# Norm multiplication and low parts of the activations on GpSimd, and another place for ScalarE's first moves, in a one-core decoder layer

## Chip, cores and metric

One core of one Trainium2 chip runs the whole layer as one program. The metric is the device time of one execution in microseconds (us); lower is better. The engines are called by the profile's names: PE (TensorE), DVE (VectorE), ACT (ScalarE), POOL (GpSimd) and SP (SyncE, whose queue issues nearly all DMAs). PEld is the weight load of PE.

## The reference, cut to what matters

The program is one conditioned decoder layer for 256 tokens of width 2048. What bears on the change is its opening: the modulation from the conditioning vector, the first norm, and the big projection `w_in` of 12288 columns.

```python
def modulate(h, shift, scale):
    return h * (1.0 + scale[:, None, :]) + shift[:, None, :]

mod = jax.nn.silu(c) @ w_ada[l] + b_ada[l]
shift1, scale1, gate1, shift2, scale2, gate2 = jnp.split(mod, 6, axis=-1)
h = modulate(rms_norm(x, g_norm1[l]), shift1, scale1)
p = h @ w_in[l]
```

All of it is float32. Behind it stand retention, HGRN2, an output projection, and a feed-forward part with a causal convolution, which the change leaves alone.

## The kernel before, in words

Activations lie transposed: 16 k tiles, each of 128 channels on the partitions and 256 tokens along the row. Four tiles `xT` hold x, four k tiles in each.

**A product in three parts.** Each float32 operand is split in two for PE. A weight block arrives by DMA in a `raw` buffer (11 of them). ACT copies it, rounded, into the upper part `wh` (L176); DVE subtracts, `wl = raw - wh` (L181, in `rest`). There are four buffers each for `wh` and `wl`. An activation tile `hT` has an upper part in its first 256 columns and a low part in the next 256. PE adds upper times `wh`, low times `wh` and upper times `wl`: L205, L206 and L210 where the tokens are on the output's rows, L221, L222 and L225 where they are on its columns. In L205 and L206 the two alternate: the low part of a k tile is read right behind its upper part.

**Where an activation tile comes from.** For each k tile, the columns of `w_ada` for scale and shift arrive in four pieces. DVE multiplies each with silu(c) and adds up (L507, "dot"): two dots give the scale, two the shift. ACT makes of them the scale `s1` (L518, L519) and the shift `t1` (L524). In `modulated`, ACT writes the upper part of `hT` (L434), then the same value unrounded into `h` (L435), and DVE writes the low part, h minus upper (L436). Before that, x is multiplied by the norm factor of its token, `rx_sb` (L497, in `times`): k tiles 0 and 1 one at a time in the opening, the later ones in seven pairs by DVE, from inside the generator `ada1`, which makes one k tile.

**The order of the work.** The first 12 column groups of `w_in` (`ATT`, of 512 columns each) are visited in turns, while the activation tiles are still being made. `visits` lays out the turns: one visit takes a group as many k tiles further as are ready by the plan (about one new tile in 11 units of work). Groups 0 to 3 are opened by hand in `run` with k tiles 0 and 1. The visits begin with group 4, at first with two k tiles, then three, then four. `self.finish(*ada[:have])` at the head of a visit traces whatever is missing of the k tiles that it needs. In this phase `self.ordered` is False: a scheduler orders the instructions by their place in the trace and by their dependencies, and a few manual ones hold it. At the end of a group's first visit ACT moves the sums from PSUM to SBUF (`take`, L880: the first moves, "p<-pg"). A first move is held behind `self.upped`, the last part that ACT made and that was traced ahead of it; both `upper` and `modulated` set `self.upped`. When the visit was a group's first, a second `finish` (L1016 and L1017) traces the k tiles of the next visit before this move. The multiplication of a pair and the dots are held behind `self.last`, the last `wl`.

POOL does almost nothing: four constants at the start and four MEMSETs of tiles that the HGRN2 part uses.

Of the kernel before, what the change touches and what calls it, by code (L numbers as in the profile page):

```python
# [12 lines left out]
F32 = mybir.dt.float32  # L13
# [3 lines left out]
AF = mybir.ActivationFunctionType  # L17
ALU = mybir.AluOpType

P = 128  # L20
D = 2048
T = 256
NT = T // P
KT = D // P
# [12 lines left out]
NOSYNC = mybir.DependencyInfo(mybir.DependencyClass.NoSync, mybir.DependencyReason.DATA)  # L37
# [23 lines left out]
class Kernel:  # L61
# [368 lines left out]
    def modulated(self, dst, x, k, sc, sh):  # L430

        act = self.nc.scalar.activation
        h = self.s1([P, T], name="h")
        self.pin(act(dst[:, :T], x, AF.Identity, bias=sh[:, k : k + 1], scale=sc[:, k : k + 1]))  # L434
        self.upped = self.pin(act(h, x, AF.Identity, bias=sh[:, k : k + 1], scale=sc[:, k : k + 1]))  # L435
        self.pin(self.nc.vector.tensor_tensor(dst[:, T:], h, dst[:, :T].bitcast(F32), ALU.subtract))  # L436

    def turn_rows(self, ps, x, k, diag, t):

# [406 lines left out]
    def run(self):  # L846
        nc, a = self.nc, self.a
        c = self.consts
# [10 lines left out]
        def act(k):  # L859
            return hT[k // 2][:, k % 2, :]  # L860

        def ada1(k):
            if k > 0 and k % 2 == 0:
                ins = self.times(k, 2, rx_sb)
                self.tc.add_manual_dep(ins.ins, self.last.ins.name, NOSYNC, reason="behind the weights traced ahead of it")
            yield from self.scale_shift("ada1", k, s1, t1, self.gn1)
            if k % 2 == 0:
                hT[k // 2] = self.blk([P, 2, 2 * T], F32R, name="hT")
            self.modulated(act(k), self.xT[k // 4][:, k % 4, :], k, s1, t1)
            yield 0.7  # L870

        accs = [self.blk([P, NT, G] if c0 in ROWS else [P, 4, T], name="p") for c0 in ATT]
        done = [0] * len(ATT)
        mms = [self.mm_rows if c0 in ROWS else self.mm_cols for c0 in ATT]

        def take(g, ps, fresh):
            for at, z in self.parts(ps, ATT[g] in ROWS):
                dst = accs[g][:, at, :]
                if fresh:
                    ins = nc.scalar.activation(dst, z, AF.Copy)  # L880
                    self.tc.add_manual_dep(ins.ins, self.upped.ins.name, NOSYNC, reason="behind the parts traced ahead of it")
                else:
                    nc.vector.tensor_tensor(dst, dst, z, ALU.add)
# [10 lines left out]
        def opening(k):  # L894
# [3 lines left out]
            return z  # L898

        ada = [None, None, *(ada1(k) for k in range(2, KT))]  # L900
        gen = first(0)
        for _ in range(2):
            next(gen)
        rx = self.token_rstd(parts)
        rx_sb = c.tile([P, T], F32, name="rx_sb")
# [6 lines left out]
        h = self.s1([P, T], name="h")  # L912
# [25 lines left out]
        h = self.s1([P, T], name="h")  # L938
# [6 lines left out]
        for g in range(RESIDENT, FIRST):  # L945
            wh, wl = self.rest(self.upper(a["wa"][g][:, 1:2, :], 1, G, shift=COLS))
            mms[g](ps[g], [(act(1), wh[:, 0, :], wl[:, 0, :])], False, True)
        begun = list(self.pieces(a["wa"][FIRST][:, 0:2, :], 2))
        stock = {g: self.load(a["wa"][g][:, 0:2, :], 2, G) for g in range(FIRST + 1, FIRST + 4)}
        for _ in range(2):  # L950
# [11 lines left out]
        def visit(g):  # L962
            return COLS if g in cols else (0, 0)
# [3 lines left out]
        def begin(kind, hb, *ins):  # L967
            att.append(self.start(kind(hb, *ins, gates)))

        def visits():  # L970
            work, g = sum(done), FIRST
            seen = list(done)
            while min(seen) < KT:
                have = min(KT, 2 + int((work - LAG) / ADA_EVERY))
                m = have - seen[g]
                if m > 0:
                    yield g, m, work
                    seen[g] = have
                    work += m
                else:  # L980
                    work += 0.5
                g = (g + 1) % len(ATT)
                if have == KT and seen[0] < KT:
                    g = min(i for i in range(len(ATT)) if seen[i] < KT)

        def early(g, m):
            k = done[g]
            pieces = self.pieces(a["wa"][g][:, k : k + m, :], m, shift=visit(g), raw=stock.pop(g, None))
            return chain([next(pieces)], pieces)

        small = False
        plan = list(visits())
# [3 lines left out]
        for n, (g, m, work) in enumerate(plan):  # L996
            if work > SMALL and not small:
                small = True
                self.small_loads(nc.sync, ("freq", "lbT", "lmask"))
                self.start(self.trig())  # L1000
                self.start(self.lower_bound())
            fresh = done[g] == 0
            have = done[g] + m
            self.finish(*ada[:have])
            bank = ps[g] if g < RESIDENT else self.pg()
            whole = g >= RESIDENT
            ahead = early(*plan[n + 1][:2]) if m <= 2 and n + 1 < len(plan) else None
            if n == 0:
                for i in range(RESIDENT, FIRST):
                    take(i, ps[i], True)  # L1010
            if g == FIRST + 2 and fresh:
                self.pace(1, 4, ADA_EVERY / 2)
            self.products(mms[g], bank, a["wa"][g], act, done[g], m, first=whole, last=whole or have == KT, shift=visit(g), begun=begun)
            done[g] = have
            begun = ahead or (early(*plan[n + 1][:2]) if n + 1 < len(plan) else None)
            if fresh and n + 1 < len(plan):  # L1016
                self.finish(*ada[: done[plan[n + 1][0]] + plan[n + 1][1]])  # L1017
            if whole or have == KT:
                take(g, bank, fresh or not whole)
            if have == KT and ATT[g] in GATES:  # L1020
                nc.scalar.activation(accs[g], accs[g], AF.Silu)
                gates[GATES.index(ATT[g])] = accs[g]
            for hb in range(2):
                gs = [hb, 2 + hb, 4 + hb]
                if g in gs and min(done[i] for i in gs) == KT:
                    self.pace(0, 14.0, 24)
                    begin(self.hgrn, hb, *(accs[i] for i in gs))
                    for i in gs:
                        accs[i] = None
# [92 lines left out]
        def half(j, t):  # L1122

            return self.modulated_half(turned[j], 2 * j, self.sc2, self.sh2, t)
# [6 lines left out]
        for t in range(NT):  # L1131
            self.residual(x1[3], ps, g, None, 3, t)
            if t == 1:
                h = half(0, 0)
# [272 lines left out]
```

## Time and profile before

| what | value |
|---|---|
| time, median of 3 runs (lowest, highest) | 1504.11 us (1503.45, 1504.54) |
| the profiled execution: its own time | 1503.49 us |
| its span, from first to last instruction | 1501.7 us |
| granted TensorE clock, mean | 0.997 |
| PE busy | 1486.4 us, 99% of the span |
| DVE busy | 1206.5 us, 80% |
| ACT busy | 835.3 us, 56% |
| POOL busy | 4.0 us, 8 instructions |

In each row of a time line stand the start of the instruction in us from the span's start, its duration (or that of a run of like instructions, with their count behind the x), the engine, the line of the kernel, the operation and its tiles as out<-in, and in square brackets how long the engine had been idle before it and who ended this. Engines overlap their instructions somewhat: a row of 1.22 us on DVE is followed by the next after 1.14 us. The end of a matmul is modelled.

### The profile page before, as it was taken

What the parts mean: (1) busy time and instruction counts of PE and PEld (TensorE: products, weight loads), DVE (VectorE), ACT (ScalarE), POOL (GpSimd) and SP (SyncE); (2) the same over time, 40 slices, a digit from 0 to 9 for tenths busy, and PEclk for the clock granted to TensorE, in tenths of its full rate; (3) what the DMA queues carried; (4) which work ended last, traced back from release to release, by engine and by line L of the source; (5) the groups of instructions that cost most, each with busy time, mean ns of one, the idle gap of its engine ahead of it and who ended that gap; (6) DMA issues with size and microseconds to landing.
All of it is one profiled execution on the core that took longest, in us unless ns stands there. A gap on an engine that the chain in (4) does not pass through costs nothing.

```text
span 1501.7 us, 22778 instructions
## 1 busy us (share of the span) xinstructions
PE 1486.4 (99%) x8529; PEld 1275.6 (85%) x8529; DVE 1206.5 (80%) x1647; ACT 835.3 (56%) x1204; POOL 4.0 (0%) x8
## 2 busy tenths in 40 slices
PE   9999999999999999999999999999999999999997
PEld 8788898888888888888888888888888888888886
DVE  7799996999999877898978778778777769455694
ACT  5646446767775644445466555555555558344342
POOL 0000000000000000000000000000000000000000
PEclk9999999999999999999999999999999999999999
DMA  9999997778887889989847777777777666666551
GB/s 364 374 336 340 317 325 261 259 259 277 277 284 265 280 299 328 314 289 363 306 131 241 249 232 233 234 234 238 232 247 233 222 188 207 196 210 209 180 186 56
DMA packets 111167, 385.73 MB, mean 257 GB/s; under 512 B 12832, under 2 KB 13392, under 8 KB 111056
## 3 DMA queue, kind: packets, MB, share of 16 engines
q1 hardware_dynamic: 110160, 383.14, 76.1%
q8 instruction: 67, 1.10, 0.3%
q10 hardware_dynamic: 896, 1.13, 0.2%
q14 instruction: 44, 0.36, 0.1%
HBM read 382.11 MB, written 2.11 MB: 256 GB/s over the span
## 4 chain that ended last, share of the span: by engine, by line
PE 91%; DVE 4%; ACT 2%; issue 1%; DMA 1%; DVEq 0%; ACTq 0%
PE pg L205 12%; PE pg L206 12%; PE pg L210 12%; PE po L1240 11%; PE pg L1240 11%; PE po L1242 5%; PE pg L1242 5%; PE pg L255 4%; PE po L205 3%; PE po L210 3%; PE po L206 3%; PE pg L258 2%; DVE wl L181 2%; DVE raw L507 2%; ACT wh L176 1%
## 5 line engine op out<-in xcount | busy, mean ns | idle before, releaser
L181 DVE TENSOR_TENSOR wl<-raw,wh 128x1024 fp32r<-128x1024 f32 (+1 forms) x531 | 630.0, 1196 | 224.3 <-ACT wh L176 215.4
L176 ACT ACTIVATE wh<-raw 128x1024 fp32r<-128x1024 f32 (+1 forms) x531 | 544.3, 1037 | 465.0 <-PE pg L206 188.0
L507 DVE SCALAR_TENSOR_TENSOR raw<-raw,sc 128x1024 f32<-128x1024 f32 (+2 forms) x194 | 233.5, 1209 | 1.7 <-DMA raw<-in_ada 1.7
L205 PE MATMUL pg<-wh,hT 128*128 128x512 f32 x512 | 202.4, 395 | 3.2 <-ACT wh L176 2.5
L206 PE MATMUL pg<-wh,hT 128*128 128x512 f32 x512 | 199.6, 390 | 0.0
L1240 PE MATMUL po<-h2T,wh 128*128 128x512 f32 x704 | 175.8, 392 | 0.0
L1240 PE MATMUL pg<-h2T,wh 128*128 128x512 f32 x688 | 172.1, 392 | 0.0
L1240 PEld LDWEIGHTS po<-h2T,wh 128*128 128x128 f32 x704 | 125.7, 188 | 21.7
L1240 PEld LDWEIGHTS pg<-h2T,wh 128*128 128x128 f32 x688 | 122.8, 188 | 21.2
L210 PE MATMUL pg<-wl,hT 128*128 128x512 f32 x512 | 138.2, 389 | 0.0
L205 PEld LDWEIGHTS pg<-wh,hT 128*128 128x128 f32 x512 | 96.1, 188 | 24.4 <-ACT wh L176 3.3
L210 PEld LDWEIGHTS pg<-wl,hT 128*128 128x128 f32 x512 | 96.1, 188 | 20.3
L206 PEld LDWEIGHTS pg<-wh,hT 128*128 128x128 f32 x512 | 96.2, 188 | 19.2
L1242 PEld LDWEIGHTS po<-h2T,wl 128*128 128x128 f32 x704 | 93.4, 188 | 7.5
L1242 PEld LDWEIGHTS pg<-h2T,wl 128*128 128x128 f32 x688 | 91.3, 188 | 7.3
L1242 PE MATMUL po<-h2T,wl 128*128 128x256 f32 x704 | 94.5, 277 | 0.0
L1242 PE MATMUL pg<-h2T,wl 128*128 128x256 f32 x688 | 92.5, 277 | 0.0
L206 PE MATMUL pg<-wh,gs 128*128 128x512 f32 x176 | 68.6, 390 | 0.0
L205 PE MATMUL pg<-wh,gs 128*128 128x512 f32 x176 | 68.5, 389 | 0.0
L205 PE MATMUL po<-wh,gs 128*128 128x512 f32 x176 | 68.5, 389 | 0.0
L206 PE MATMUL po<-wh,gs 128*128 128x512 f32 x176 | 68.5, 389 | 0.0
L1253 ACT ACTIVATE u<-uy,convw 128x256 f32<-128x256 f32 x88 | 52.4, 595 | 28.6 <-DVE uy L1251 28.4
(275 smaller groups left out, 2025.0 us busy)
## 6 DMA issues: line engine op xcount, KB each, us to landing
raw<-in_wup SPq DMA_DIRECT2D x176, 512.0 KB, 4.6
raw<-in_wdown SPq DMA_DIRECT2D x88, 512.0 KB, 3.5
raw<-in_wa SPq DMA_DIRECT2D x81, 512.0 KB, 5.6
raw<-in_ada SPq DMA_DIRECT2D x64, 512.0 KB, 5.8
raw<-in_wab SPq DMA_DIRECT2D x64, 512.0 KB, 5.2
raw<-in_ada SPq DMA_DIRECT2D x62, 512.5 KB, 5.8
raw<-in_gate SPq DMA_DIRECT2D x32, 512.5 KB, 5.1
raw<-in_wk SPq DMA_DIRECT2D x32, 512.0 KB, 5.1
```

Source lines behind the costliest of these rows:

```text
L176: self.upped = self.pin(self.nc.scalar.activation(wh, raw, AF.Copy))
L181: self.last = self.nc.vector.tensor_tensor(wl, raw, wh.bitcast(F32), ALU.subtract)
L205: nc.tensor.matmul(ps[t], lhsT=act[:, hi], rhs=wh, start=first and i == 0, stop=False)
L206: nc.tensor.matmul(ps[t], lhsT=act[:, lo], rhs=wh, start=False, stop=False)
L210: nc.tensor.matmul(ps[t], lhsT=act[:, hi], rhs=wl, start=False, stop=last and i == len(items) - 1)
L255: nc.tensor.matmul(ps[z], lhsT=wh[:, z * P : (z + 1) * P], rhs=act, start=first and i == 0, stop=False)
L258: nc.tensor.matmul(ps[z][:, :T], lhsT=wl[:, z * P : (z + 1) * P], rhs=act[:, :T], start=False, stop=last and i == len(items) - 1)
L507: dot = self.pin(nc.vector.scalar_tensor_tensor(raw[:, 0, :], raw[:, 0, :], 1.0, self.sc[:, at:to], ALU.mult, ALU.mult, accum_out=part[:, ...
L1240: self.pin(nc.tensor.matmul(ps[z], lhsT=wh[:, z * P : (z + 1) * P], rhs=act, start=kt == 0, stop=False, skip_group_check=bool(begun)))
L1242: nc.tensor.matmul(ps[z][:, :T], lhsT=wl[:, z * P : (z + 1) * P], rhs=act[:, :T], start=False, stop=kt == KT - 1, skip_group_check=bool(be ...
L1253: nc.scalar.activation(u, y, AF.Identity, bias=w[3], scale=w[2])
```

## The change

- POOL multiplies x by the norm factor for k tiles 2 to 15, in seven instructions of two k tiles (128x512). They no longer stand in `ada1` but in `run`, behind the upper parts of groups 2 and 3. They read `rx_late`, a copy of `rx_sb` that ACT makes at that place (one instruction more on ACT).
- The low parts of the activations of k tiles 2 to 15 (14 instructions of 128x256) go from DVE to POOL.
- `modulated` no longer sets `self.upped`: the first moves are held behind upper parts of weights alone.
- The second `finish`, behind a first visit, is gone.

```diff
         self.pin(act(dst[:, :T], x, AF.Identity, bias=sh[:, k : k + 1], scale=sc[:, k : k + 1]))
-        self.upped = self.pin(act(h, x, AF.Identity, bias=sh[:, k : k + 1], scale=sc[:, k : k + 1]))
-        self.pin(self.nc.vector.tensor_tensor(dst[:, T:], h, dst[:, :T].bitcast(F32), ALU.subtract))
+        self.pin(act(h, x, AF.Identity, bias=sh[:, k : k + 1], scale=sc[:, k : k + 1]))
+        self.nc.gpsimd.tensor_tensor(dst[:, T:], h, dst[:, :T].bitcast(F32), ALU.subtract)
...
         def ada1(k):
-            if k > 0 and k % 2 == 0:
-                ins = self.times(k, 2, rx_sb)
-                self.tc.add_manual_dep(ins.ins, self.last.ins.name, NOSYNC, reason="behind the weights traced ahead of it")
             yield from self.scale_shift("ada1", k, s1, t1, self.gn1)
...
+        rx_late = c.tile([P, T], F32, name="rx_late")
+        self.pin(nc.scalar.activation(rx_late, rx_sb, AF.Copy))
+        for k in range(2, KT, 2):
+            x = self.xT[k // 4][:, k % 4 : k % 4 + 2, :]
+            nc.gpsimd.tensor_tensor(x, x, rx_late[:, None, :].to_broadcast([P, 2, T]), ALU.mult)
         begun = list(self.pieces(a["wa"][FIRST][:, 0:2, :], 2))
...
-            if fresh and n + 1 < len(plan):
-                self.finish(*ada[: done[plan[n + 1][0]] + plan[n + 1][1]])
             if whole or have == KT:
                 take(g, bank, fresh or not whole)
```

The order of PE's matmuls and of SP's DMA issues is the same in both programs. What moves is on ACT, DVE and POOL. On ACT, where k tile 2 is made (`pg_415` in the first rows and `pg_423` in the second are the same sums, of group 6; `t_166`, `hT` and `h` belong to k tile 2; the last row is the weight part that PE takes next), there stood before:

```order
L880 ACTIVATE p_174<-pg_397 128x1024
L518 ACTIVATE s_165<-dot_78_370 128x1
L519 ACTIVATE s_165<-gn_83,s_165 128x1
L524 ACTIVATE t_166<-dot_87_434 128x1
L434 ACTIVATE hT_442<-xT_113,t_166,s_165 128x256
L435 ACTIVATE h_443<-xT_113,t_166,s_165 128x256
L880 ACTIVATE p_175<-pg_415 128x1024
L176 ACTIVATE wh_467<-raw_465 128x512
```

and now there stands:

```order
L877 ACTIVATE p_174<-pg_405 128x1024
L518 ACTIVATE s_165<-dot_78_378 128x1
L519 ACTIVATE s_165<-gn_83,s_165 128x1
L877 ACTIVATE p_175<-pg_423 128x1024
L524 ACTIVATE t_166<-dot_87_442 128x1
L434 ACTIVATE hT_451<-xT_113,t_166,s_165 128x256
L435 ACTIVATE h_452<-xT_113,t_166,s_165 128x256
L176 ACTIVATE wh_475<-raw_473 128x512
```

The move of group 6 has gone from behind the activations of k tile 2 to ahead of their shift; where k tile 3 is made, the move of group 9 goes the same way. On ACT at k tile 8, where a table load and the sine and cosine of the rotary angles fall in (`t_166`, `hT` and `h` are of k tile 8), there stood before:

```order
L176 ACTIVATE wh_1327<-raw_1325 128x1024
L524 ACTIVATE t_166<-dot_220_1303 128x1
L434 ACTIVATE hT_1335<-xT_115,t_166,s_165 128x256
L435 ACTIVATE h_1336<-xT_115,t_166,s_165 128x256
L176 ACTIVATE wh_1371<-raw_1369 128x1024
L572 ACTIVATE n_1236<-ang_1235 128x256
L573 ACT_TABLE_LOAD
L573 ACTIVATE sin<-ang_1235 128x256
L574 ACTIVATE cos<-n_1236,halfpi 128x256
L176 ACTIVATE wh_1404<-raw_1402 128x1024
```

and now there stands:

```order
L176 ACTIVATE wh_1332<-raw_1330 128x1024
L572 ACTIVATE n_1241<-ang_1240 128x256
L573 ACT_TABLE_LOAD
L573 ACTIVATE sin<-ang_1240 128x256
L574 ACTIVATE cos<-n_1241,halfpi 128x256
L524 ACTIVATE t_166<-dot_220_1308 128x1
L434 ACTIVATE hT_1340<-xT_115,t_166,s_165 128x256
L435 ACTIVATE h_1341<-xT_115,t_166,s_165 128x256
L176 ACTIVATE wh_1376<-raw_1374 128x1024
L176 ACTIVATE wh_1409<-raw_1407 128x1024
```

The four instructions for the angles have gone from between two weight parts to ahead of the shift of k tile 8. On DVE, right behind the opening (`wl` are low parts of weights, the dots with `dot_87` and `dot_93` those of the shift of k tile 2 and the scale of k tile 3), there stood before:

```order
L181 TENSOR_TENSOR wl_360<-raw_357,wh_359 128x1024
L497 TENSOR_TENSOR xT_113<-xT_113,rx_sb 128x512
L181 TENSOR_TENSOR wl_379<-raw_363,wh_378 128x1024
L181 TENSOR_TENSOR wl_399<-raw_365,wh_398 128x1024
L507 SCALAR_TENSOR_TENSOR raw_371,dot_78_370<-raw_371,sc 128x1024
L181 TENSOR_TENSOR wl_417<-raw_367,wh_416 128x1024
L507 SCALAR_TENSOR_TENSOR raw_374,dot_78_370<-raw_374,sc 128x1025
L507 SCALAR_TENSOR_TENSOR raw_435,dot_87_434<-raw_435,sc 128x1024
L507 SCALAR_TENSOR_TENSOR raw_438,dot_87_434<-raw_438,sc 128x1025
L507 SCALAR_TENSOR_TENSOR raw_462,dot_93_461<-raw_462,sc 128x1024
L436 TENSOR_TENSOR hT_442<-h_443,hT_442 128x256
L181 TENSOR_TENSOR wl_468<-raw_465,wh_467 128x512
```

and now there stands:

```order
L181 TENSOR_TENSOR wl_369<-raw_366,wh_368 128x1024
L181 TENSOR_TENSOR wl_387<-raw_372,wh_386 128x1024
L181 TENSOR_TENSOR wl_407<-raw_374,wh_406 128x1024
L507 SCALAR_TENSOR_TENSOR raw_379,dot_78_378<-raw_379,sc 128x1024
L181 TENSOR_TENSOR wl_425<-raw_376,wh_424 128x1024
L507 SCALAR_TENSOR_TENSOR raw_382,dot_78_378<-raw_382,sc 128x1025
L507 SCALAR_TENSOR_TENSOR raw_443,dot_87_442<-raw_443,sc 128x1024
L507 SCALAR_TENSOR_TENSOR raw_447,dot_87_442<-raw_447,sc 128x1025
L507 SCALAR_TENSOR_TENSOR raw_470,dot_93_469<-raw_470,sc 128x1024
L181 TENSOR_TENSOR wl_476<-raw_473,wh_475 128x512
```

The multiplication of the first pair and the low part of k tile 2 are gone from DVE; the rest stands as before. In POOL's queue the seven multiplications and then the 14 low parts stand ahead of the four MEMSETs.

## The prediction

> **What bounds the kernel now.** I read the page first, then PE's waits in the phase that the change touches, then the time lines of PE, ACT and DVE around those waits. From the page:
>
> ```profile
> PE 1486.4 (99%) x8529; PEld 1275.6 (85%) x8529; DVE 1206.5 (80%) x1647; ACT 835.3 (56%) x1204; POOL 4.0 (0%) x8
> ```
>
> PE is idle for 15.3 of 1501.7 us. The order of its matmuls does not change, so a gain can only come out of idle time of PE; a loss has no such end. PE's waits from 0 to 450 us, which holds the visits (line, who ended the wait, us in total, times, the longest):
>
> ```profile
> PE pg L205 <- ACT wh L176: 2.5, 2, 1.5
> PE pg L221 <- ACT wh L176: 1.0, 2, 0.7
> PE pg L205 <- DVE p L883: 0.6, 1, 0.6
> ```
>
> The other rows there are of the opening, which stands ahead of the first moved instruction, or are 0.3 us and less. So 3.5 us hang on ACT's upper parts of weights and 0.6 us on a DVE addition. PE's time line shows the two waits on L205, with the ends of the groups ahead of them:
>
> ```profile
> 38.38 1.07 PE L210 MATMUL pg<-wl,hT 128*128 128x512 f32 x4
> ...
> 41.10 1.07 PE L210 MATMUL pg<-wl,hT 128*128 128x512 f32 x4
> 43.16 0.50 PE L205 MATMUL pg<-wh,hT 128*128 128x512 f32 x1 [1.00 <-ACT wh L176]
> 43.50 0.39 PE L206 MATMUL pg<-wh,hT 128*128 128x512 f32 x1
> ...
> 52.37 0.62 PE L210 MATMUL pg<-wl,hT 128*128 128x512 f32 x2
> ...
> 54.64 1.07 PE L210 MATMUL pg<-wl,hT 128*128 128x512 f32 x4
> 57.20 0.50 PE L205 MATMUL pg<-wh,hT 128*128 128x512 f32 x1 [1.50 <-ACT wh L176]
> ```
>
> and ACT's time line shows why the weight part was late:
>
> ```profile
> 40.26 0.29 ACT L524 ACTIVATE t<-dot 128x1 f32<-128x1 f32 x1 [1.58 <-DVE raw L507]
> 40.59 0.60 ACT L434 ACTIVATE hT<-xT,t,s 128x256 fp32r<-128x256 f32 x1
> 41.10 0.59 ACT L435 ACTIVATE h<-xT,t,s 128x256 f32<-128x256 f32 x1
> 41.59 1.01 ACT L880 ACTIVATE p<-pg 128x1024 f32<-128x1024 f32 x1
> 42.49 1.57 ACT L176 ACTIVATE wh<-raw 128x512 fp32r<-128x512 f32 x2
> ...
> 53.88 0.29 ACT L524 ACTIVATE t<-dot 128x1 f32<-128x1 f32 x1 [2.44 <-DVE raw L507]
> ...
> 55.21 1.00 ACT L880 ACTIVATE p<-pg 128x1024 f32<-128x1024 f32 x1
> 56.11 1.99 ACT L176 ACTIVATE wh<-raw 128x1024 fp32r<-128x1024 f32 x2
> ```
>
> ACT sat idle until DVE's last shift dot, made the activation, and then did a first move that could have been done while it was idle, ahead of the weight part that PE was waiting for.
>
> **The change part by part.** First the moves. At k tile 2 the move's sums are complete at 38.38 + 1.07 = 39.45, inside ACT's idle 1.58 us. Now ahead of the shift, it takes ACT from 39.45 for 0.90 us (from 41.59 to 42.49 in the rows), to 40.35. The shift starts at 40.35 in place of 40.26; from it to the weight part are then only 41.59 - 40.26 = 1.33 us, so the weight part starts at 41.68, 0.81 us earlier than 42.49. PE follows at 42.35 and had been free from 41.10 + 1.07 = 42.17: 0.8 of the 1.0 us is gained. At k tile 3 the sums are complete at 52.37 + 0.62 = 52.99, inside the idle 2.44 us; the move is over at 53.9, the shift is held up by 0.02 us, and the weight part starts at 55.23 in place of 56.11. PE would start at 56.32 and is free from 55.71: 0.9 of 1.5 us gained. Everything in between is paced by PE's own groups and slides with it. Together **-1.7 us**.
>
> The other wait on ACT, at k tile 8:
>
> ```profile
> 131.40 0.29 ACT L524 ACTIVATE t<-dot 128x1 f32<-128x1 f32 x1 [4.34 <-DVE raw L507]
> ...
> 134.10 1.28 ACT L573 ACT_TABLE_LOAD   x1
> ...
> 136.12 1.04 ACT L176 ACTIVATE wh<-raw 128x1024 fp32r<-128x1024 f32 x1
> ```
>
> and on PE:
>
> ```profile
> 133.83 0.38 PE L221 MATMUL pg<-hT,wh 128*128 128x256 f32 x1 [0.68 <-ACT wh L176]
> ...
> 137.22 0.39 PE L221 MATMUL pg<-hT,wh 128*128 128x256 f32 x1 [0.34 <-ACT wh L176]
> ```
>
> The angles and the table load, 2.4 us of ACT between two weight parts, now stand ahead of the shift, in an idle stretch of 4.34 us. The second wait (0.34) goes. But DVE must have made the angles first, some 2.4 us ahead of its shift dot, else the shift, and PE's first wait with it, grows by up to about 1 us. I take **0**, between -0.3 and +0.7.
>
> The second `finish` traces nothing new and PE's order is unmoved; all that it did to ACT is in the moves above. The copy `rx_late` stands ahead of this row:
>
> ```profile
> 27.22 1.06 ACT L176 ACTIVATE wh<-raw 128x1024 fp32r<-128x1024 f32 x1 [0.72 <-DVE hT L943]
> ```
>
> It is as large as L434 above, which holds ACT for 0.5 us (40.59 to 41.10), and fits into the 0.72: nothing. Without that cover it would cost 0.5.
>
> What leaves DVE, by form from 27 to 262 us (count, busy us, mean ns), and the nearest row of POOL:
>
> ```profile
> L436 DVE TENSOR_TENSOR hT<-h,hT 128x256 fp32r<-128x256 f32 x14 | 5.9, 420 | 1.1 <-ACT h L435 1.0
> L497 DVE TENSOR_TENSOR xT<-xT,rx_sb 128x512 f32<-128x512 f32 x7 | 4.8, 683 | 0.0
> ...
> L644 POOL MEMSET at<- 128x1024 f32 x2 | 1.9, 957 | 291.6 <-PE po L765 178.0 <-DMA raw<-in_wa 113.6
> ```
>
> That is 10.7 us of DVE. It brings PE nothing directly: only 0.6 us of PE's waits here name DVE.
>
> What POOL needs for the same work no row shows. From below I take DVE's 0.68 and 0.42 us. From above: a MEMSET writes 1024 elements in 0.957 us; three such passes (two reads, one write) over 512 elements are 1.44 us, over 256 are 0.72. The seven multiplications start behind `rx_late` at about 27.2 and take 4.8 to 10.1 us, so they end by 37.3; the first reader is L434 at 40.6, the next pair is read from 68.4 on. The low part of k tile 2 can start when `h` ends, at 41.78, and PE reads it in the L206 that follows its L205 by 43.50 - 43.16 = 0.34 us, at 42.69: 0.9 us of room, and both bounds fit. At k tile 3, PE runs k tile 2's pair first, so there is more. The MEMSETs, now behind the low parts, are late by up to 125 us (from 114 to behind k tile 15, near 239), and the first reader of such a tile comes after 300 us: nothing.
>
> The sum is -1.7 + 0 + 0, on the profiled execution's own 1503.49 us: 1501.8. That execution lies 0.6 us below the median 1504.11; the same difference from the median gives 1502.4, and I say **1502.5**. A measurement of this kernel can tell about 0.2%, 3 us, from no change: this gain lies within.
>
> **The rivals.** *POOL holds up DVE.* Both engines read two SBUF operands per element in all that matters here. In the trace of before POOL only writes, four times 0.96 us, so nothing speaks for or against. The place is the stretch of DVE behind the opening:
>
> ```profile
> 27.14 2.42 DVE L181 TENSOR_TENSOR wl<-raw,wh 128x512 fp32r<-128x512 f32 x3
> 29.48 0.68 DVE L497 TENSOR_TENSOR xT<-xT,rx_sb 128x512 f32<-128x512 f32 x1
> 30.08 1.22 DVE L181 TENSOR_TENSOR wl<-raw,wh 128x1024 fp32r<-128x1024 f32 x1
> 33.28 1.23 DVE L181 TENSOR_TENSOR wl<-raw,wh 128x1024 fp32r<-128x1024 f32 x1 [1.98 <-ACT wh L176]
> ...
> 39.00 1.22 DVE L507 SCALAR_TENSOR_TENSOR raw<-raw,sc 128x1025 f32<-128x1025 f32 x1
> 40.15 0.08 DVE L507 DVE_READ_ACCUMULATOR raw<-raw,sc 128x1 f32 x1
> ```
>
> From 27.14 to the shift dot's end at 40.23, DVE idles for 2 us alone, and that dot releases ACT and then PE. If each of the seven multiplications stops DVE for its own length, between the bounds 1.06 us, that is 7.4 us; less 0.6 for the multiplication that is gone from the row at 29.48, less about half of the idle time: the dot ends 5.8 us later. The weight part of k tile 2 no longer has the move ahead of it (-0.9), so PE restarts 4.9 us later than at 43.16; k tile 3 gives back 0.9 as above. Price +4.0: 1508.1. It crosses zero once the dot is late by more than 1.8 us. Ends: 0.68 us each with all the idle time used, +0.4 (1504.5); 1.44 us each with none, +7.7 (1511.8). The low parts add little where DVE waits for ACT anyway.
>
> The Trainium skill states this as a rule (SBUF — State Buffer, Who interferes with whom): a DVE instruction with two SBUF inputs contends with a GpSimd instruction that reads SBUF, and whichever starts first blocks the other for its whole length. No run here shows it, and it speaks against this change. The same skill (GPSIMD Engine Reference, 3.1) has 4497 ns for a GpSimd tensor_tensor of 2048 elements; an estimate from it is 1.1 us for each multiplication, and by both pages the time would be near 1508.
>
> *DVE's relief counts after all.* If the dots come earlier because DVE has 10.7 us less to do, all waits in the three rows may go: 3.5 + 0.6 = 4.1 us, 1500.0. Against it: ahead of both L205 waits DVE itself waits for ACT's weight parts, which wait for PE.
>
> *The moves do nothing for PE,* because POOL's low part takes the weight part's place as what comes last. Beyond 0.9 us of room, each further us costs PE one at k tile 2; at 1.7 us for a low part the 0.8 gained there is gone, and the time is 1503.3. Both bounds speak against it.
>
> **How the numbers follow.** The forecast with its own range 1500.8 to 1504.0 (the third wait and POOL's bounds), and the rival of the low part beside it: 0.48, of which 0.02 is for later low parts or the angles costing PE over 3 us. DVE held up: 0.38, of which 0.04 ends within 3 us of before. DVE's relief: 0.14, below 1501.1. Hence faster by over 0.2%: 0.14; within 0.2%: 0.46 + 0.04 = 0.50; slower: 0.34 + 0.02 = 0.36. The range runs from 1500.8, which leaves out the better part of the relief, to 1510.0, which takes in the rival up to multiplications of about 1.3 us: 1500.8 to 1510.0, with less than 2 in 10 outside.
>
> **What would show it.** Right: PE's waits at 43 and 57 us shrink to about 0.2 and 0.6, the rows L880 stand ahead of L524 with ACT idle before them, and DVE's rows between 27 and 40 us keep their 0.68 and 1.22 us. The rival: DVE rows in that stretch grow, or gaps open between them, while POOL multiplies, and PE's wait near 43 us grows to 5 us. The forecast is wrong if the sum of PE's waits before 450 us moves by more than 3 us either way.

## The result and the profile after

The changed kernel takes **1511.29 us** (median of 4 runs, 1510.83 to 1512.0), the kernel before on the same chip 1503.78 us (4 runs, 1503.32 to 1504.54): a ratio of 1.005, 95% interval 1.0032 to 1.0067. It is slower by 7.5 us. Ratios and intervals, here and below, leave out three runs in a slow state (one of e9, two of the kernel before) and are not exactly the quotients of the medians. The profiled execution has a span of 1510.2 us against 1501.7, which is 8.5 us more. The forecast of 1502.5 was wrong in its sign, and the time lies 1.3 us above the range. What happened is the first rival, *POOL holds up DVE*, at about twice its price.

The first part of the page of after; engines, busy us, share of the span, instructions:

```profile
PE 1491.5 (99%) x8529; PEld 1280.0 (85%) x8529; DVE 1207.8 (80%) x1626; ACT 835.4 (55%) x1205; POOL 30.1 (2%) x29
```

DVE has 21 instructions less than before and is busy 1.3 us longer. Work was taken from it, so what is left must have become slower. DVE's groups by form from 24 to 41 us show it (form and count, then busy us and mean ns of one, then idle time ahead). First before:

```profile
L181 DVE TENSOR_TENSOR wl<-raw,wh 128x1024 fp32r<-128x1024 f32 x4 | 4.9, 1221 | 2.0 <-ACT wh L176 2.0
L507 DVE SCALAR_TENSOR_TENSOR raw<-raw,sc 128x1024 f32<-128x1024 f32 x3 | 3.7, 1220 | 0.0
L181 DVE TENSOR_TENSOR wl<-raw,wh 128x512 fp32r<-128x512 f32 x4 | 2.6, 686 | 0.0
L507 DVE SCALAR_TENSOR_TENSOR raw<-raw,sc 128x513 f32<-128x513 f32 x1 | 0.7, 691 | 0.0
L943 DVE TENSOR_TENSOR hT<-h,hT 128x256 fp32r<-128x256 f32 x1 | 0.4, 421 | 0.0
```

and after (L940 there is the instruction of L943 before):

```profile
L181 DVE TENSOR_TENSOR wl<-raw,wh 128x1024 fp32r<-128x1024 f32 x4 | 8.0, 2034 | 0.0
L181 DVE TENSOR_TENSOR wl<-raw,wh 128x512 fp32r<-128x512 f32 x4 | 4.8, 1229 | 0.0
L507 DVE SCALAR_TENSOR_TENSOR raw<-raw,sc 128x1024 f32<-128x1024 f32 x1 | 2.3, 2308 | 0.0
L940 DVE TENSOR_TENSOR hT<-h,hT 128x256 fp32r<-128x256 f32 x1 | 1.5, 1515 | 0.0
L507 DVE SCALAR_TENSOR_TENSOR raw<-raw,sc 128x513 f32<-128x513 f32 x1 | 0.7, 691 | 0.0
```

The dot of 513 columns, which runs at 23.9 us, ahead of POOL, keeps its 691 ns. The rows beside POOL grow: on the average by 0.81 for the four wide low parts and by 0.54 for the four narrow ones, by 1.09 for the dot (2308 against 1220 of its form before) and by 1.09 for L940 (1515 against 421). That is 7.6 us, made by seven rows of 1.09 each, as many as there are multiplications; three wide and two narrow low parts are among them. The idle 2.0 us are gone too. And POOL multiplies in just that stretch (POOL's time line):

```profile
26.92 12.86 POOL L949 TENSOR_TENSOR xT<-xT,rx_late 128x512 f32<-128x512 f32 x7 [26.48 <-ACT rx_late L946]
47.03 0.72 POOL L436 TENSOR_TENSOR hT<-h,hT 128x256 fp32r<-128x256 f32 x1 [7.26 <-ACT h L435]
```

Behind 39.8 us DVE's rows are 1.21 to 1.22 us again. But the lateness stays. The last shift dot of k tile 2 on DVE (it ended at 40.23 before), and what ACT does behind it:

```profile
44.22 1.22 DVE L507 SCALAR_TENSOR_TENSOR raw<-raw,sc 128x1025 f32<-128x1025 f32 x1
45.36 0.08 DVE L507 DVE_READ_ACCUMULATOR raw<-raw,sc 128x1 f32 x1
```

```profile
43.80 1.00 ACT L877 ACTIVATE p<-pg 128x1024 f32<-128x1024 f32 x1
45.47 0.30 ACT L524 ACTIVATE t<-dot 128x1 f32<-128x1 f32 x1 [0.67 <-DVE raw L507]
45.86 0.60 ACT L434 ACTIVATE hT<-xT,t,s 128x256 fp32r<-128x256 f32 x1
46.37 0.58 ACT L435 ACTIVATE h<-xT,t,s 128x256 f32<-128x256 f32 x1
46.86 1.56 ACT L176 ACTIVATE wh<-raw 128x512 fp32r<-128x512 f32 x2
```

The first move (L877, L880 before) does stand ahead of the shift, as predicted. But the dot ends at 45.44, 5.2 us later: 7.6 us less the idle 2.0 and the 0.6 of the multiplication that DVE no longer has, and 0.2 by which DVE was behind already when POOL began. The weight part starts 4.4 us later than at 42.49. PE's time line:

```profile
42.58 1.07 PE L210 MATMUL pg<-wl,hT 128*128 128x512 f32 x4
47.53 0.80 PE L205 MATMUL pg<-wh,hT 128*128 128x512 f32 x1 [3.88 <-ACT wh L176]
48.12 0.63 PE L206 MATMUL pg<-wh,hT 128*128 128x512 f32 x1
...
52.82 0.63 PE L205 MATMUL pg<-wh,hT 128*128 128x512 f32 x1
...
54.46 0.39 PE L205 MATMUL pg<-wh,hT 128*128 128x512 f32 x1
...
63.45 0.50 PE L205 MATMUL pg<-wh,hT 128*128 128x512 f32 x1 [0.65 <-ACT wh L176]
78.75 0.39 PE L222 MATMUL po<-hT,wh 128*128 128x256 f32 x1 [0.81 <-POOL hT L436]
```

There are two losses here. PE restarts at 47.53 and not at 43.16. (It was 1.5 us late ahead of the wait already, 1.1 of it from its opening; that costs nothing by itself, because the dot ends the wait.) And the same matmuls then take 0.63 us in place of 0.39 until about 53.5. The stretches of PE (us, busy us and matmuls, granted clock, DMA share, GB/s) say why:

```profile
44.00:48.00 4.00, 0.47 (x1) 0.82 1.03 361
48.00:52.00 4.00, 4.00 (x11) 0.50 0.98 370
52.00:56.00 4.00, 4.00 (x16) 0.83 1.00 373
56.00:60.00 4.00, 4.00 (x20) 1.00 0.89 323
```

After the standstill the granted clock is 0.50 for some microseconds. Matched one by one, the n-th matmul of after against the n-th of before, the lateness grows like this: +4.4 at the restart, +2.6 over the 13 matmuls at half clock, -0.85 at k tile 3 (wait 0.65 and not 1.50), +1.3 at k tile 4 (for the most part the row at 78.75, which waits for POOL's low part), +0.9 around k tile 8. From 142 us to the end it is constant at 8.4 to 8.5 us. The sum is 8.4, and all of the loss is made in the first tenth of the span.

### The profile page after: what moved, and what is told of

It is laid out like the page before. It is cut to its first block, busy times and chain, and to the rows that moved or that the text cites. A ratio compares the mean times of both kernels' runs of the same rounds, so it can differ in the third digit from the quotient of the medians.

```text
span 1510.2 us, 22786 instructions
## 1 busy us (share of the span) xinstructions
PE 1491.5 (99%) x8529; PEld 1280.0 (85%) x8529; DVE 1207.8 (80%) x1626; ACT 835.4 (55%) x1205; POOL 30.1 (2%) x29
## 4 chain that ended last, share of the span: by engine, by line
PE 92%; DVE 3%; ACT 2%; DMA 2%; issue 1%; SPq 0%; DVEq 0%; POOL 0%; ACTq 0%
PE pg L205 13%; PE pg L206 13%; PE pg L210 12%; PE po L1240 11%; PE pg L1240 10%; PE po L1242 5%; PE pg L1242 5%; PE pg L255 4%; PE po L210 3%; PE po L205 3%; PE po L206 3%; PE pg L258 2%; DVE wl L181 1%; DVE raw L507 1%; PE pg L225 1%
```

## The experiments

*The theory:* POOL's instructions hold up DVE's, because both read SBUF, and DVE's last shift dot is on PE's path; the half clock behind the standstill adds to it. *The rivals:* the new place of the first moves and of the angles costs the time; POOL's low parts are late; or POOL is late with its data. The runs of before that each kernel is compared with have medians of 1503.62 (e1 to e4), 1503.81 (e5 to e8) and 1503.63 us (e9 and e10).

### The parts of the change, one at a time

**e1: before with the two edits of the order alone.** POOL as before.

```diff
-        self.upped = self.pin(act(h, x, AF.Identity, bias=sh[:, k : k + 1], scale=sc[:, k : k + 1]))
+        self.pin(act(h, x, AF.Identity, bias=sh[:, k : k + 1], scale=sc[:, k : k + 1]))
...
-            if fresh and n + 1 < len(plan):
-                self.finish(*ada[: done[plan[n + 1][0]] + plan[n + 1][1]])
```

> The kernel before with only the two edits on the order: modulated no longer marks the part that the first moves are held behind, and the second finish is gone. All elementwise work stays on DVE. Theory (POOL holds up DVE, and the moves by themselves are a gain): PE's waits on L205 near 43 and 57 us fall from 1.0 and 1.5 us to about 0.2 and 0.6, the wait pair at k tile 8 stays at 1.0, and the time is 1.2 to 2.0 us under before, about 1502.2. Rival (the loss is made by the new order on ACT): over 1506. Rival (the moves do nothing): 1503.5 to 1504.5.

Measured: 1503.68 us, ratio 1.0001 (0.9991 to 1.001). PE's time line at the three places:

```profile
42.48 0.50 PE L205 MATMUL pg<-wh,hT 128*128 128x512 f32 x1 [0.23 <-ACT wh L176]
55.68 0.50 PE L205 MATMUL pg<-wh,hT 128*128 128x512 f32 x1 [0.65 <-ACT wh L176]
70.71 0.39 PE L222 MATMUL po<-hT,wh 128*128 128x256 f32 x1 [0.60 <-DVE hT L436]
```

The waits are the 0.2 and 0.6 that the prediction worked out, and 0.77 and 0.85 us are gained. But a new wait stands at k tile 4, and a further loss of 0.7 us at 103 us. From 105 us on PE is 0.4 us behind before, and from 135 us on level with it. ACT's rows near 100 us show one of the two changes of order that came with the edits:

```profile
99.68 0.30 ACT L524 ACTIVATE t<-dot 128x1 f32<-128x1 f32 x1 [5.57 <-DVE raw L507]
99.89 1.05 ACT L176 ACTIVATE wh<-raw 128x1024 fp32r<-128x1024 f32 x1
100.84 0.58 ACT L434 ACTIVATE hT<-xT,t,s 128x256 fp32r<-128x256 f32 x1
```

A weight part stands between the shift and the activation of k tile 6; before, the activation came first. e9 and e10 test whether that order is the cause.

**e2: after, with the low parts back on DVE.**

```diff
-        self.nc.gpsimd.tensor_tensor(dst[:, T:], h, dst[:, :T].bitcast(F32), ALU.subtract)
+        self.pin(self.nc.vector.tensor_tensor(dst[:, T:], h, dst[:, :T].bitcast(F32), ALU.subtract))
```

> The changed kernel, with the low parts back on DVE: the seven multiplications alone are on POOL. Theory (the multiplications hold up DVE between 27 and 40 us): the five DVE rows in that stretch take about 2 us each as in the changed kernel, PE waits about 3.9 us near 43 to 47 us, the granted clock drops behind it, and the time is 1508 to 1510; it is under the changed kernel by the 1 to 2 us that PE waits or is held up for low parts from 78 us on. Rival (the low parts make the loss): 1502 to 1503.

Measured: 1511.01 us, ratio 1.0046 (1.0031 to 1.0061): nearly all of the loss, without one low part on POOL. PE's row is

```profile
47.32 0.80 PE L205 MATMUL pg<-wh,hT 128*128 128x512 f32 x1 [4.28 <-ACT wh L176]
```

The time lies 1 us above the range that was expected: putting the low parts back on DVE saves 0.3 us and not 1 to 2. The wait at k tile 4 is there as well, 0.56 us for DVE's low part, against 0.81 for POOL's in after.

**e3: after, with the multiplications back on DVE** and back in `ada1`, as before. The moves and POOL's low parts stay.

```diff
+            if k > 0 and k % 2 == 0:
+                ins = self.times(k, 2, rx_sb)
+                self.tc.add_manual_dep(ins.ins, self.last.ins.name, NOSYNC, reason="behind the weights traced ahead of it")
...
-        rx_late = c.tile([P, T], F32, name="rx_late")
-        self.pin(nc.scalar.activation(rx_late, rx_sb, AF.Copy))
-        for k in range(2, KT, 2):
-            x = self.xT[k // 4][:, k % 4 : k % 4 + 2, :]
-            nc.gpsimd.tensor_tensor(x, x, rx_late[:, None, :].to_broadcast([P, 2, T]), ALU.mult)
```

> The changed kernel, with the multiplications back on DVE inside ada1: the 14 low parts alone are on POOL. Theory (the multiplications make most of the loss): the first wait near 43 us is 0.2 to 0.5, no drop of the clock there, and PE waits for a low part once or twice by 0.3 to 1 us each: 1502.5 to 1504.5. Rival (the low parts make the loss): 1508 and more.

Measured: 1503.88 us, ratio 1.0004 (0.9994 to 1.0013). By the matmuls one by one it is 0.35 us behind e1. So the loss belongs to the multiplications.

### What the half clock costs

**e4: after, with 8 matmuls more in PE's wait.** They multiply ones by a tile of zeros and add that to sums already there, ahead of the first use of k tile 2.

```diff
+            if self.fill and k0 + kt == 2:
+                for _ in range(self.fill):
+                    self.nc.tensor.matmul(ps[0][:, :P], lhsT=self.zeros, rhs=self.ones, start=False, stop=False, skip_group_check=True)
+                self.fill = 0
...
+        self.zeros = c.tile([P, P], F32, name="zeros")
+        nc.vector.memset(self.zeros, 0.0)
```

> The changed kernel, with eight matmuls of a tile of zeros added to the open sums of PE right ahead of the first use of k tile 2, so that PE works for about 3.3 of the 3.9 us that it waits there; nothing else is moved. Theory (the granted clock halves because PE stood still for almost 4 us): no half clock behind the wait, the 13 matmuls that were slowed by 0.2 us each are not, and the time is 2 to 2.6 us under the changed kernel, about 1508.9. Rival (the half clock comes for another reason, or at a fixed time): the half clock stays near 47 to 53 us and the time is that of the changed kernel, 1511.3.

Measured: 1509.84 us, ratio 1.0041 (1.0026 to 1.0056). PE's time line (lines of the kernel are one higher here):

```profile
43.13 1.95 PE L289 MATMUL pg<-ones,zeros 128*128 128x128 f32 x16
47.56 0.50 PE L206 MATMUL pg<-wh,hT 128*128 128x512 f32 x1 [2.49 <-ACT wh L177]
47.90 0.46 PE L207 MATMUL pg<-wh,hT 128*128 128x512 f32 x1
48.20 0.39 PE L206 MATMUL pg<-wh,hT 128*128 128x512 f32 x1
```

PE restarts as late as in after, but at 0.39 us per matmul. The 8 matmuls fill 1.95 us of the wait, not the 3.3 that were expected. The 13 matmuls that lost 2.6 us lose 0.07. The profiled span is 1507.6 us, 2.6 below after's; the medians are 1.45 apart, less than the 2 to 2.6 that were expected, so of the half clock's share 1.5 to 2.6 us are seen.

### POOL beside DVE, with nothing else changed

**e5: before, with seven multiplications on POOL into a tile that nobody reads.** One more copy on ACT lets them start where after's do; DVE keeps all its work.

```diff
+        aside = c.tile([P, 2, T], F32, name="aside")
+        self.pin(nc.scalar.activation(aside[:, 0, :], rx_sb, AF.Copy))
+        for _ in range(7):
+            nc.gpsimd.tensor_tensor(aside, self.xT[3][:, 0:2, :], rx_sb[:, None, :].to_broadcast([P, 2, T]), ALU.mult)
```

> The kernel before, with seven multiplications of 128x512 added on POOL at the place where the changed kernel has its own; they write a tile that nobody reads, so no instruction depends on them. Theory (POOL's reading holds up DVE, whatever becomes of the product): the DVE rows from 27 to 40 us take about twice their time as in the changed kernel, PE waits 4 us and more near 43 to 48 us with half the clock behind it, and the time is 7 to 9 us over before, 1511 to 1513. Rival (PE waits for products of POOL): 1503.5 to 1504.5.

Measured: 1511.17 us, ratio 1.0052 (1.0034 to 1.007). DVE's groups from 24 to 41 us:

```profile
L181 DVE TENSOR_TENSOR wl<-raw,wh 128x1024 fp32r<-128x1024 f32 x3 | 6.9, 2320 | 0.0
L497 DVE TENSOR_TENSOR xT<-xT,rx_sb 128x512 f32<-128x512 f32 x1 | 1.8, 1796 | 0.0
```

Nobody waits for these seven results, and the loss is there in full: DVE's rows are 1.1 us longer (2320 against 1221, 1796 against 683). PE's row is

```profile
49.14 0.80 PE L205 MATMUL pg<-wh,hT 128*128 128x512 f32 x1 [5.12 <-ACT wh L176]
```

So the cause is neither late data nor the order.

**e6: the same place, 26 MEMSETs of 128x512,** which write but read nothing.

```diff
-        for _ in range(7):
-            nc.gpsimd.tensor_tensor(aside, self.xT[3][:, 0:2, :], rx_sb[:, None, :].to_broadcast([P, 2, T]), ALU.mult)
+        for _ in range(26):
+            nc.gpsimd.memset(aside, 0.0)
```

> The kernel before, with 26 MEMSETs of 128x512 added on POOL at the same place: POOL writes for some 13 us and reads nothing. Theory (it is reading that holds up DVE): DVE's rows keep their 0.68 and 1.22 us, and the time is within 0.7 us of before, 1503.0 to 1504.3. Rival (any work of POOL holds up DVE, by its writes too): 1508 and more.

Measured: 1503.80 us, ratio 0.9999 (0.999 to 1.0009). DVE's groups in the same window:

```profile
L181 DVE TENSOR_TENSOR wl<-raw,wh 128x1024 fp32r<-128x1024 f32 x4 | 4.9, 1222 | 2.4 <-ACT wh L176 2.4
L497 DVE TENSOR_TENSOR xT<-xT,rx_sb 128x512 f32<-128x512 f32 x1 | 0.7, 683 | 0.0
```

Not one row has grown, though POOL is busy until 42 us.

**e7: the same place, 20 copies of 128x512,** which read one operand.

```diff
-        for _ in range(7):
-            nc.gpsimd.tensor_tensor(aside, self.xT[3][:, 0:2, :], rx_sb[:, None, :].to_broadcast([P, 2, T]), ALU.mult)
+        for _ in range(20):
+            nc.gpsimd.tensor_copy(aside, self.xT[3][:, 0:2, :])
```

> The kernel before, with 20 copies of 128x512 added on POOL at the same place, each reading one operand. Theory (reading holds up DVE): DVE's rows from 27 us on grow while POOL copies, by up to the length of a copy each; if POOL is busy for 10 us or more the time is 3 to 9 us over before. Rival (only two-operand work of POOL collides): DVE's rows keep their length and the time is 1503.0 to 1504.3.

Measured: 1508.34 us, ratio 1.0029 (1.0018 to 1.0041). DVE's groups again:

```profile
L181 DVE TENSOR_TENSOR wl<-raw,wh 128x1024 fp32r<-128x1024 f32 x4 | 6.4, 1626 | 0.0
L497 DVE TENSOR_TENSOR xT<-xT,rx_sb 128x512 f32<-128x512 f32 x1 | 1.1, 1094 | 0.0
```

Each DVE instruction beside a copy is 0.41 us longer, against 1.1 beside a multiplication. A copy that DVE does not hold up takes

```profile
45.66 0.62 POOL L951 COPY aside<-xT 128x512 f32<-128x512 f32 x1
```

From writing only over one operand to two, the cost goes 0, 0.41, 1.1 us, while POOL's own instruction takes 0.53, 0.62 and 1.29 us where it is not held up (the last is in e8). So it is POOL's reading that costs DVE, and where POOL reads, a DVE row grows by POOL's own length less 0.2 us. Whether the number of operands has a part in the price besides the length was not tried.

### Ways to keep something of it

**e8: after, but the pairs spread out.** The first pair stays on DVE; each of the six others stands in POOL's queue behind the low part of the k tile before it.

```diff
+            if k == 2:
+                ins = self.times(k, 2, rx_sb)
+                self.tc.add_manual_dep(ins.ins, self.last.ins.name, NOSYNC, reason="behind the weights traced ahead of it")
+            elif k % 2 == 0:
+                x = self.xT[k // 4][:, k % 4 : k % 4 + 2, :]
+                ins = nc.gpsimd.tensor_tensor(x, x, rx_sb[:, None, :].to_broadcast([P, 2, T]), ALU.mult)
+                self.tc.add_manual_dep(ins.ins, self.low.ins.name, NOSYNC, reason="behind the low part of the k tile before")
```

> The changed kernel with the first pair multiplied on DVE as before, and each of the six other pairs multiplied on POOL right behind the low part of the k tile before it, in place of all seven at once from 27 us. Theory (what cost so much was seven in a row in the stretch of DVE that PE waits for next): no long wait near 43 us, no half clock there, the two waits near 43 and 57 us stay at 0.2 and 0.7, single collisions cost PE under 1 us each, and the time is that of the low parts alone, 1503.5 to 1505.5. Rival (each collision costs PE its length wherever it is): 1508 to 1512.

Measured: 1504.41 us, ratio 1.0006 (0.9997 to 1.0016). The multiplications collide here as well. POOL's time line:

```profile
56.37 1.29 POOL L868 TENSOR_TENSOR xT<-xT,rx_sb 128x512 f32<-128x512 f32 x1
...
86.57 2.28 POOL L868 TENSOR_TENSOR xT<-xT,rx_sb 128x512 f32<-128x512 f32 x1
```

One that DVE holds up takes 2.28 us, one that it does not hold up 1.29. Not every row of DVE takes part. This one, which runs while the second of these multiplies, adds sums in PSUM to a tile in SBUF, and so reads one operand from SBUF:

```profile
87.62 1.21 DVE L887 TENSOR_TENSOR p<-p,pg 128x1024 f32<-128x1024 f32 x1
```

It takes the 1.21 us that L883 takes in before, where POOL stands still. One at a time, spread over 200 us, the multiplications cost little: the median is 0.5 us above that of e3, which has the same edits without them. What hurt was seven in a row in the one stretch whose last instruction PE waits for. Nothing is gained either: DVE's relief brings nothing that these times show.

**e9: the two moves, with the later order put back.** The first weight part traced behind an activation is held behind it on ACT, and the first move of group 11 comes one visit later.

```diff
+        if getattr(self, 'made', None) is not None:
+            self.tc.add_manual_dep(self.upped.ins, self.made.ins.name, NOSYNC, reason='behind the activation traced ahead of it')
+            self.made = None
...
-            if fresh and n + 1 < len(plan):
-                self.finish(*ada[: done[plan[n + 1][0]] + plan[n + 1][1]])
-            if whole or have == KT:
+            if late:
+                take(*late.pop())
+            if fresh and g == len(ATT) - 1:
+                late.append((g, bank, True))
+            elif whole or have == KT:
```

> The program of before without the second finish (its place alone gives the order of e1_moves), and with three holds that put the later k tiles back: the first weight part traced behind an activation is held behind that activation on ACT, and the first move of group 11 is made one visit later in the trace. On ACT the first moves of groups 6 and 9 stand ahead of the shifts of k tiles 2 and 3; at k tile 4 the order of ACT and DVE is that of before, at k tile 6 too. Theory (the 1.6 us were given back because the order of ACT and DVE at k tiles 4 and 6 changed with the moves): PE's waits near 42.5 and 55.7 us are 0.2 and 0.6, the waits of 0.6 us near 71 and 0.5 us near 103 of e1_moves are gone, PE stands 1.5 to 1.7 us ahead of before from 57 to 120 us, and the time is 1502.1 (-1.7 to -1.2, unless k tile 8, where the angles again stand ahead of the shift, costs up to 0.9). Rival (DVE's dots of k tile 4 are the next thing late, whatever the order): waits of 0.5 us and more appear near 71 us all the same and the time is that of before within 0.4 us.

Measured: 1504.41 us, ratio 1.0002 (0.9993 to 1.0012). PE's waits of 0.2 us and more between 38 and 215 us:

```profile
43.28 0.50 PE L208 MATMUL pg<-wh,hT 128*128 128x512 f32 x1 [0.23 <-ACT wh L176]
56.46 0.50 PE L208 MATMUL pg<-wh,hT 128*128 128x512 f32 x1 [0.65 <-ACT wh L176]
134.43 0.39 PE L224 MATMUL pg<-hT,wh 128*128 128x256 f32 x1 [1.37 <-ACT wh L176]
195.70 0.39 PE L224 MATMUL po<-hT,wh 128*128 128x256 f32 x1 [0.81 <-ACT wh L176]
```

The wait at 71 us is gone, as the order theory said, and the 1.6 us last until 103 us: PE stands 0.9 us behind before at 42 us (its opening was slower in this execution) and 0.7 ahead of it from 57 to 100. But the total did not come out. 0.4 us are lost near 103 and 1.1 at 195 us, where ACT's weight part of k tile 12 waits for a dot that comes 0.85 us later than before. The lowering of the time by 1.2 to 1.7 us that was expected isn't there. The gain goes back piece by piece. That another order on ACT or DVE does it each time is argued here and not shown.

**e10: one first move alone.** The second `finish` is left out behind the visits of groups 4 to 8 only.

```diff
-            if fresh and n + 1 < len(plan):
+            if fresh and g > 8 and n + 1 < len(plan):
```

> The program of before with the second finish left out behind the visits of groups 4 to 8 alone, so that one first move changes its place, that of group 6 ahead of the shift of k tile 2; every other row of ACT, DVE and PE stands as before. Theory (a first move ahead of the shift is worth what ACT's rows say, and is given back only where an order changes behind it): PE's wait near 42.5 us is 0.2 in place of 1.0, and the 0.8 us stay to the end: 1503.0, 0.8 below the runs of before beside it. Rival (what follows is late by itself): the wait near 57 us grows from 1.5 to 2.3 us, or one near 71 us appears, and the time is that of before within 0.2 us.

Measured: 1502.96 us, ratio 0.9995 (0.9986 to 1.0004). PE's time line:

```profile
42.38 0.50 PE L205 MATMUL pg<-wh,hT 128*128 128x512 f32 x1 [0.23 <-ACT wh L176]
56.45 0.50 PE L205 MATMUL pg<-wh,hT 128*128 128x512 f32 x1 [1.50 <-ACT wh L176]
```

The wait at 42 us is 0.23 and not 1.00, the next is unchanged at 1.50, and PE stays 0.6 to 0.8 us ahead of before from 43 us to the last matmuls. Where no other row changes its place, the gain that ACT's rows promise is kept. The median is 0.7 us below before's and 8.3 below after's, the lowest of all kernels here; but the interval holds 1, so that it beats before isn't shown by the times.

## Why the prediction was wrong, point by point

- **The step that failed** is the third term, the work given to POOL at a price of 0. The prediction saw the collision as a rival at 0.38, and put the forecast on rows in which POOL does not read at all. Its words there were right: the trace spoke neither for nor against. With e2, e5 and e6 the cause is shown: seven multiplications on POOL that read SBUF, without any data passing, make a loss of the full size (7.4 us in e5), and 26 instructions that only write make none. The Trainium skill's rule (SBUF — State Buffer, Who interferes with whom), which the prediction cited as speaking against the change, holds in each of these runs: two SBUF inputs on DVE collide with a GpSimd instruction that reads, not with one that writes. That the other is blocked for the whole length comes out to within 0.2 us: 1.09 of 1.29 us, 0.41 of 0.62. The rival should have had the larger chance.
- **The rival's own steps** were nearly right in kind. 1.06 us for each multiplication: measured 1.09. That these are so near is in part luck: the 1.06 was the middle of two bounds for POOL's own length, which is 1.29 where DVE does not hold it up. The dot 5.8 us later: measured 5.2. All of the idle 2.0 us was used up, not half. PE's restart 4.9 us later: measured 4.4.
- **What the rival's price lacked** is the half clock behind the standstill, 2.6 us in the profiled runs (e4 takes it away). The trace of before had waits of 1.0 and 1.5 us alone, and behind neither is the clock reduced. It also lacked the 1.3 us at k tile 4 and the 0.9 at k tile 8 (see the next three points). Hence the upper end of 1510.0, 1.3 us short.
- **The first term, the moves** at -1.7, failed too. The waits came out as 0.23 and 0.65, as worked out, in e1. What failed is "slides with it". ACT and DVE did not keep their order at k tiles 4 and 6, and the 1.6 us were given back. e10, whose order is otherwise unchanged, keeps its 0.8; in e9 the wait at k tile 4 goes with the order, but other places give the gain back.
- **The angles** at k tile 8, 0 with up to 0.7: in after about 0.9 us are lost around there, 0.2 more than the upper bound; in e9 with the same order of the angles the balance from 122 to 142 us is zero. What makes the difference is not shown; the new order of the angles was not tried alone.
- **POOL's low parts**: 0.72 to 0.75 us alone, at the upper bound of 0.72, inside the room of 0.9 at k tile 2. At k tile 4 there was no such room: 0.81 us of wait on POOL, which the rival of the low part had placed at k tile 2. But most of it is not POOL's: with the low part on DVE the wait is there too, 0.60 us in e1 and 0.56 in e2, so it came with the moves. Over the whole of k tile 4 PE loses 1.3 us in after and 1.0 in e1. e3 has the sum: 0.35 us net against e1.

## What to carry to other kernels

Work on an idle POOL isn't free if it reads SBUF while DVE reads two operands there: look at which engine's rows stand beside it, and at what waits for the last of them, before moving work there. Spread such work, one instruction at a time, away from the stretch that releases the engine that bounds the kernel. A gain on that engine's wait is only kept as long as the other engines keep their order behind it, so compare the rows of the next stages, not just of the one that is mended.

## What the runs showed of the hardware

- POOL beside DVE, per DVE instruction with two SBUF inputs: +1.09 to 1.1 us for a two-operand 128x512, +0.41 for a one-operand copy, 0 for a MEMSET. These instructions of POOL take 1.29, 0.62 and 0.53 us where they are not held up. POOL pays too: the multiplication takes up to 2.28 us beside DVE, the copy up to 1.49. A DVE addition with one input in SBUF and one in PSUM keeps its 1.21 us beside a multiplication (e8, 87.62 us).
- PE's clock falls in a wait of 3.8 to 5.1 us: in after, e2, e5 and e7 the records show 0.50 for about 6.8 us, of which the first part still lies in the wait. After waits of 1.0 and 1.5 us (before, e6) nothing falls, and in e4, where 8 small matmuls (16 in the records) cut the idle stretch to 2.49 us, nothing does either. The Trainium skill (TensorE: Matmul & The Clock Gate, Part 1) has an idle window of about 3.4 us for this, and half clock until a busy window of that length has passed; the lengths of the waits here agree with it on both sides, and 6.8 us is twice its window. The moment does not agree: the clock falls 2.0 us (e5) to 3.1 us (e7) behind the modelled end of the last matmul.
- A long wait is not the only thing that lowers the clock. In the opening the records show 0.50 from 15.3 to 18.7 us in before and from 12.4 to 19.2 us in after, with PE's waits in the 10 us ahead of it at 0.6 us and less. What lowers it there is not shown.
- The price of a quiet stretch of PE is therefore not its length alone: behind the wait of 1.5 us in before no matmul is slowed, and behind that of 3.9 us in after PE loses 2.6 us more.
